# Hybrid decoder layer: the third and fourth right side of the MLP's up projection, tied on VectorE behind the second weights of its first two pairs

## The chip, the cores and the metric

The kernel runs on one core of a Trainium2 chip, as one program. The time is the device time of one execution in microseconds (us). Before the change it is 1497.02 us, the median of three executions (1496.89 to 1497.15).

The core has five engines with a queue of instructions each, and each works through its own queue in order: TensorE (PE in the profile, with its weight loads as PEld), VectorE (DVE), ScalarE (ACT), GpSimd (POOL) and SyncE (SP, which here issues every transfer). They meet at semaphores alone.

## The reference

One layer of a hybrid decoder on 1024 tokens of width 1024, all in float32. Ahead of the MLP stand an mLSTM and a forgetting attention side by side, and a cross attention into 256 memory tokens. The last part is

```python
        x = x + cross_attention(rmsnorm(x, ln_x[l]), rmsnorm(mem, ln_mem[l]), w_xq[l], w_xkv[l], w_xo[l])

        u = jax.nn.relu(rmsnorm(x, ln2[l]) @ w_ff1[l])
        x = x + (u * u) @ w_ff2[l]
    return rmsnorm(x, ln_f)
```

with `w_ff1` 1024 x 4096 and `w_ff2` 4096 x 1024. The change touches the step from the output projection of the cross attention (`w_xo`) into the up projection (`w_ff1`).

## The kernel before

**Numbers in two parts.** A float32 operand is kept as two tiles, `hi` and `lo`. `split` (L135) makes them: ScalarE copies the source into `hi` with rounding (L138), then VectorE subtracts `hi` from the source into `lo` (L139). A product is three matmuls, `lo*hi`, `hi*lo`, `hi*hi` (`mm3`, L221 to L223). So weights that come from memory cost one ACT and one DVE instruction of 128 x 1024 for each tile before TensorE can use them, and TensorE asks for the `lo` part first (L221).

**The up projection in seven products.** The normalised input (1024 x 1024, transposed) is cut into four blocks: y11 and y12 are the first 512 features for the first and the second 512 tokens, y21 and y22 the other 512 features. The weights are handled in 16 pairs of column tiles. For a pair, instead of eight block products seven are made, with sums and differences of blocks on both sides. The right sides (the table `RIGHTS`, L1474) are `11`, `21`, `t1`, `t2`, `22`, `t3` and `t4`, each an `act` tile of four k-slices of 512, hi and lo. Product i of pair p is called job (p, i) here. `jobs` (L1477) gives TensorE's order: for the first two pairs (0,1) (1,1) (0,2) (1,2) (0,5) (1,5) (0,6) (1,6) (0,3) (1,3) (0,7) (1,7) (0,4) (1,4). A job is four k-slices of three matmuls.

**Where the right sides come from.** `xo_sink` (L1506) adds each tile of `w_xo`'s output to the residual (L1509), squares it for the norm (ACT L258, DVE L262) and writes the scaled tile into `ys` (L1513). Right sides 11 and 21 are split while the first 512 tokens run, `t1` and `t2` (a `sub`, L1428, and a split for each k) while the second 512 tokens run, tile by tile (L1595, L1596). What is left then, in the list `rest` (L1612), is four splits for `22`, four times `third` and four times `fourth`:

- `third(k)`: y12 = y22 - y12 on VectorE (L1428), then a split into `t3` (ACT L138, DVE L139).
- `fourth(k)`: y21 = y21 - y11 on VectorE, then a split into `t4`.

`t3` is used first by job (0,7), `t4` by job (0,4): the last but one and the last product of a pair.

**Where the weights come from.** `left_up(p, group)` (L1449) makes the left sides of a pair in three groups: group 0 for jobs 1 and 2 (and 4), group 1 for jobs 5 and 6, group 2 for jobs 7 and 3. Each group is one 128 x 1024 split into tiles `wh` and `wl`, three buffers each for the whole kernel. "The second weights" are group 1. Group 0 of pair 1 adds five VectorE operations on 512 columns that build the sums (L1462 to L1467); from pair 2 on they run on GpSimd.

**What sets the order.** The program is recorded as the loops run; a scheduler then merges the recorded instructions into one queue for each engine, by priority in the order of recording, by readiness in its own estimate of time, and by free buffers. A manual dependence without a semaphore (`add_manual_dep` with `NoSync`) only says that one instruction has to stand behind another on an engine. The loop over jobs (L1723) records, ahead of each job, the weights of five jobs further on (`prepare`, L1491) and one or two entries of `rest`.

**Behind that stage**, `Pair.run` (L1629) adds up the products of a pair on VectorE (L1627), ScalarE makes relu and square (L1616, L1617), and `put_right` and `put` (L1663, L1670) split the results and write them to memory for the down projection, two DVE instructions of L139 and L1428 kind after another, while the next pairs run. The down projection (L1788) and the last part (L1865) follow.

Of the kernel before, what the change touches and what calls it, by code (L numbers as in the profile page):

```python
# [44 lines left out]
def hybrid_layer(ctx: ExitStack, tc: tile.TileContext, a: dict, out: bass.AP):  # L45
    nc = tc.nc
# [12 lines left out]
    def sb(tag, shape, bufs, dt=F32):  # L59
        return pool.tile(shape, dt, tag=tag, name=name(tag), bufs=bufs)  # L60
# [18 lines left out]
    def w2(tag, n=512, dt=F32, p=P):  # L79
        return sb("r_" + tag, [P, 512], BUFS[tag], dt)[:p, :n]  # L80
# [54 lines left out]
    def split(hi, lo, src, scale=None):  # L135

        if scale is None:
            s.activation(hi, src, AF.Copy)  # L138
            return v.tensor_tensor(out=lo, in0=src, in1=hi.bitcast(F32), op=ALU.subtract)  # L139
        else:  # L140
            s.activation(hi, src, AF.Copy, scale=scale)
            return v.scalar_tensor_tensor(out=lo, in0=src, scalar=scale, in1=hi.bitcast(F32), op0=ALU.mult, op1=ALU.subtract)
# [82 lines left out]
    def both(pair, f):  # L225
        return f(pair[0]), f(pair[1])
# [77 lines left out]
    at = 0  # L304
# [950 lines left out]
    fourth = []  # L1255
# [171 lines left out]
    def sub(out_, x, y, by=v):  # L1427
        by.tensor_tensor(out=out_, in0=x, in1=y, op=ALU.subtract)  # L1428
# [8 lines left out]
    def raw_pair(p_, n0, n1):  # L1437
        raws = [sb("wr", [P, 1024], 2) if p_ % 2 else z4()[:, :1024] for _ in range(2)]
        if p_ > 1:
            n0, n1 = n1, n0  # L1440
        for raw, n in zip(raws, (n0, n1)):
            load(raw, a["w_ff1"][n])
        return raws[::-1] if p_ > 1 else raws

    todo = [(b, k, 4 * b + k, 4 * b + 2 + k) for b in range(NB) for k in range(2)]

    cuts = {}

    def left_up(p_, group):  # L1449

        if group == 0:
            raws[p_] = raw_pair(p_, *todo[p_][2:])
        r1, r2 = raws[p_]
        x11, x12, x21, x22 = r1[:, :TH], r1[:, TH:], r2[:, :TH], r2[:, TH:]
        hi, lo = (sb(t, [P, 1024], 3, F32R) for t in ("wh", "wl"))
        split(hi, lo, (r1, r2, r1)[group])
        if group == 0:
            h22, l22 = (w2(t, dt=F32R) for t in ("bc" if p_ else "ay"))
            split(h22, l22, x22)
            cuts[p_, 4] = both((h22, l22), lambda t: t.rearrange("p (k c) -> p k c", k=4))  # L1460

            by = g if p_ > 1 else v  # L1462
            by.tensor_tensor(out=x21, in0=x21, in1=x22, op=ALU.add)
            sub(x22, x21, x11, by)
            sub(x12, x12, x22, by)
            sub(x11, h22.bitcast(F32), x22, by)
            by.tensor_tensor(out=x11, in0=x11, in1=l22.bitcast(F32), op=ALU.add)  # L1467
        for e in range(2):
            cuts[p_, ((1, 2), (5, 6), (7, 3))[group][e]] = both((hi, lo), lambda t: t[:, e * TH : e * TH + TH].rearrange("p (k c) -> p k c", k=4))
        if group == 2:  # L1470
            del raws[p_]
# [11 lines left out]
    first = {}  # L1483
# [7 lines left out]
    def prepare(at):  # L1491
        while prep and first[prep[0]] <= at + LEAD:
            left_up(*prep.pop(0))

    def cut_h(c, hf, ks=range(4)):
        k0 = 4 if c in ("21", "22", "t4") else 0
        for k in ks:
            ins = split(H[c][0][:, k], H[c][1][:, k], ys[hf][k0 + k])
        return ins
# [86 lines left out]
    for n in range(KT):  # L1586
        w = weights(a["w_xo"][n])
        if n == 1:
            norm_factors(0)
        if n in (1, 7):  # L1590
            left_up(*prep.pop(0))
        for _, _, ps in proj(w, os_, 1, order=[(1, 0)]):
            xo_sink(n, 1, ps)
        k = n % 4
        sub(ys[0][k], ys[1][n], ys[0][k])  # L1595
        cut_h("t2" if n > 3 else "t1", 0, (k,))  # L1596
# [3 lines left out]
    def third(k):  # L1600
        y12, y22 = parts[1][k], parts[3][k]
        sub(y12, y22, y12)
        cut_h("t3", 1, (k,))

    def fourth(k):

        y11, y21 = parts[0][k], parts[2][k]
        sub(y21, y21, y11)
        cut_h("t4", 0, (k,))


    rest = [lambda k=k: cut_h("22", 1, (k,)) for k in range(4)] + [lambda k=k: third(k) for k in range(4)] + [lambda k=k: fourth(k) for k in range(4)]  # L1612

    def squared(x, y):

# [105 lines left out]
    pairs = {}  # L1721
    later = []
    for at, (p_, i) in enumerate(jobs):  # L1723
# [14 lines left out]
        if i == 4:  # L1738
            b, k = todo[p_][:2]
# [207 lines left out]
```

## Time and profile before

| | value |
|---|---|
| median of three executions | 1497.02 us |
| profiled execution: its own time | 1498.83 us |
| profiled execution: span of the trace | 1497.1 us, 22496 instructions |
| PE busy | 1479.4 us, 99% of the span |
| PEld busy | 1253.1 us, 84% |
| DVE busy | 1131.0 us, 76% |
| ACT busy | 773.1 us, 52% |
| POOL busy | 521.2 us, 35% |
| granted TensorE clock | 0.998 |

Of a profile row in time order, the first number is the start in us from the span's start, the second the duration, then engine, line, operation, output and inputs by the program's names without buffer numbers; in brackets stands the idle time of that engine just before, and who ended it. Neighbouring rows of one form are merged (x2). The end of a matmul is modelled and overlaps the next one, so a gap between matmuls is read from their starts. The output projection of the second 512 tokens runs until about 849 us of the span, the up projection from about 841 us to past 1150 us, and the down projection after it.

### The profile page before, as it was taken

What the parts mean: (1) busy time and instruction counts of PE and PEld (TensorE: products, weight loads), DVE (VectorE), ACT (ScalarE), POOL (GpSimd) and SP (SyncE); (2) the same over time, 40 slices, a digit from 0 to 9 for tenths busy, and PEclk for the clock granted to TensorE, in tenths of its full rate; (3) what the DMA queues carried; (4) which work ended last, traced back from release to release, by engine and by line L of the source; (5) the groups of instructions that cost most, each with busy time, mean ns of one, the idle gap of its engine ahead of it and who ended that gap; (6) DMA issues with size and microseconds to landing.
All of it is one profiled execution on the core that took longest, in us unless ns stands there. A gap on an engine that the chain in (4) does not pass through costs nothing. (4 is left out here: it accounts for less than half of the span.)

```text
span 1497.1 us, 22496 instructions
## 1 busy us (share of the span) xinstructions
PE 1479.4 (99%) x7790; PEld 1253.1 (84%) x7790; DVE 1131.0 (76%) x1867; ACT 773.1 (52%) x1492; POOL 521.2 (35%) x552
## 2 busy tenths in 40 slices
PE   9999999999999999999999999999999999999997
PEld 9988888889999888889988787888888888888887
DVE  7775776776798875677668888999996677787665
ACT  7434353445688664577644557666665521222134
POOL 1002020414456441633200045454544365553312
PEclk9999999999999999999999999999999999999999
DMA  6422333446778867744544447776678767776623
GB/s 231 138 95 69 130 97 134 132 132 191 247 242 284 285 231 247 261 168 128 167 165 155 139 171 268 253 246 238 233 267 304 264 260 281 281 274 253 250 87 113
DMA packets 125878, 303.58 MB, mean 203 GB/s; under 512 B 14898, under 2 KB 30060, under 8 KB 118852
## 3 DMA queue, kind: packets, MB, share of 16 engines
q1 hardware_dynamic: 125764, 302.15, 57.9%
q8 instruction: 61, 1.00, 0.3%
q14 instruction: 53, 0.43, 0.1%
HBM read 203.28 MB, written 98.82 MB: 202 GB/s over the span
## 5 line engine op out<-in xcount | busy, mean ns | idle before, releaser
L221 PE MATMUL tp<-act,wl 128*128 128x512 f32 (+1 forms) x440 | 172.7, 392 | 0.0
L222 PE MATMUL tp<-act,wh 128*128 128x512 f32 (+1 forms) x440 | 172.2, 391 | 0.0
L223 PE MATMUL tp<-act,wh 128*128 128x512 f32 (+1 forms) x440 | 171.7, 391 | 0.0
L139 DVE TENSOR_TENSOR wl<-wr,wh 128x1024 fp32r<-128x1024 f32 (+2 forms) x99 | 131.8, 1331 | 29.0 <-ACT wh L138 28.7
L138 ACT ACTIVATE wh<-wr 128x1024 fp32r<-128x1024 f32 (+2 forms) x99 | 99.9, 1010 | 86.3 <-PE tp L223 28.9
L221 PE MATMUL mm<-act,wl 128*128 128x512 f32 (+1 forms) x332 | 123.7, 373 | 0.0
L223 PE MATMUL mm<-act,wh 128*128 128x512 f32 (+1 forms) x332 | 123.5, 372 | 0.0
L222 PE MATMUL mm<-act,wh 128*128 128x512 f32 (+1 forms) x332 | 123.5, 372 | 0.0
L221 PE MATMUL m<-act,wl 128*128 128x512 f32 (+1 forms) x308 | 113.9, 370 | 1.8 <-DVE wl L139 1.8
L223 PE MATMUL m<-act,wh 128*128 128x512 f32 (+1 forms) x308 | 113.7, 369 | 0.0
L222 PE MATMUL m<-act,wh 128*128 128x512 f32 (+1 forms) x308 | 113.4, 368 | 0.0
L223 PE MATMUL sc<-act,wh 128*128 128x512 f32 (+1 forms) x280 | 105.6, 377 | 0.0
L221 PE MATMUL sc<-act,wl 128*128 128x512 f32 (+1 forms) x280 | 105.5, 377 | 0.0
L222 PE MATMUL sc<-act,wh 128*128 128x512 f32 (+1 forms) x280 | 105.5, 377 | 0.0
L223 PEld LDWEIGHTS tp<-act,wh 128*128 128x128 f32 x440 | 82.7, 188 | 18.6
L221 PEld LDWEIGHTS tp<-act,wl 128*128 128x128 f32 x440 | 82.7, 188 | 18.5 <-DVE r_f L1627 0.2
L222 PEld LDWEIGHTS tp<-act,wh 128*128 128x128 f32 x440 | 82.8, 188 | 18.2
L1711 POOL TENSOR_TENSOR z<-wr 128x256 f32<-128x256 f32 x56 | 50.1, 915 | 135.6 <-DMA wr<-w_ff2q 133.1
L138 ACT ACTIVATE wh<-z 128x1024 fp32r<-128x1024 f32 (+1 forms) x54 | 55.4, 1026 | 79.0 <-POOL z L1711 58.4
L139 DVE TENSOR_TENSOR wl<-z,wh 128x1024 fp32r<-128x1024 f32 (+1 forms) x54 | 79.3, 1468 | 9.3 <-ACT wh L138 9.3
L138 ACT ACTIVATE w<-wr 128x768 fp32r<-128x768 f32 (+3 forms) x35 | 28.1, 802 | 109.5 <-PE tp L221 33.5
L223 PEld LDWEIGHTS mm<-act,wh 128*128 128x128 f32 x332 | 62.4, 188 | 11.7
(793 smaller groups left out, 4398.5 us busy)
## 6 DMA issues: line engine op xcount, KB each, us to landing
act<-right SPq DMA_DIRECT2D x49, 1024.0 KB
right<-w SPq DMA_DIRECT2D x56, 256.0 KB
wr<-w_ff2q SPq DMA_DIRECT2D x28, 512.0 KB
right<-r_d SPq DMA_DIRECT2D x49, 256.0 KB
right<-r_e SPq DMA_DIRECT2D x49, 256.0 KB
act<-fqk SPq DMA_DIRECT2D x48, 256.0 KB
wr<-w_in SPq DMA_DIRECT2D x20, 512.0 KB
wr<-w_ff SPq DMA_DIRECT2D x20, 512.0 KB
```

The costliest lines, as they stand in the source:

```text
L138: s.activation(hi, src, AF.Copy)
L139: return v.tensor_tensor(out=lo, in0=src, in1=hi.bitcast(F32), op=ALU.subtract)
L221: nc.tensor.matmul(ps, w[1], x[0], start=first, stop=False, skip_group_check=more)
L222: nc.tensor.matmul(ps, w[0], x[1], start=False, stop=False, skip_group_check=more)
L223: nc.tensor.matmul(ps, w[0], x[0], start=False, stop=last, skip_group_check=more)
L1711: g.tensor_tensor(out=o, in0=x, in1=y, op=op)
```

## The change

`left_up` now keeps, for each pair and group, the VectorE instruction that writes the `lo` tile. The eight entries of `rest` for `third` and `fourth` are recorded through a new function, which adds a manual dependence without a semaphore from each of their VectorE instructions to the `lo` instruction of pair 1, group 1. Only VectorE's instructions are tied. No instruction is added or taken away.

```diff
-    cuts = {}
+    cuts, cut_of = {}, {}
...
-        split(hi, lo, (r1, r2, r1)[group])
+        cut_of[p_, group] = split(hi, lo, (r1, r2, r1)[group])
...
+    def later_than(cut, do):
+        at = len(nc.cur_bb.bb.instructions)
+        do()
+        for i in nc.cur_bb.bb.instructions[at:]:
+            if i.engine == mybir.EngineType.DVE:
+                tc.add_manual_dep(
+                    i,
+                    cut_of[cut].ins.name,
+                    mybir.DependencyInfo(mybir.DependencyClass.NoSync, mybir.DependencyReason.DATA),
+                    reason="behind the weights of the first pairs",
+                )
+
-    rest = [lambda k=k: cut_h("22", 1, (k,)) for k in range(4)] + [lambda k=k: third(k) for k in range(4)] + [lambda k=k: fourth(k) for k in range(4)]
+    rest = [lambda k=k: cut_h("22", 1, (k,)) for k in range(4)] + [lambda f=f, k=k: later_than((1, 1), lambda: f(k)) for f in (third, fourth) for k in range(4)]
```

The scheduler then plans everything behind that point anew. Three places of VectorE's queue show it. In the rows the last number of a name is the tile's own number; lines above L1612 stand 12 higher in the changed file (L1627 is L1639).

VectorE before, up to the `lo` part of pair 0's group 1 (`wl_9589`), which job (0,5) asks for. `act_9585` is `t3`, `act_9586` is `t4`, `act_9200` is `t2`:

```order
L1428 TENSOR_TENSOR w_1680_9154<-w_1680_9154,w_1653_8987 128x512
L139 TENSOR_TENSOR act_9585<-w_1694_9237,act_9585 128x512
L1509 TENSOR_TENSOR r_p_9572<-mm_9547,r_p_9572 128x512
L139 TENSOR_TENSOR act_9585<-w_1694_9237,act_9585 128x512
L1428 TENSOR_TENSOR wr_9530<-wr_9530,wr_9531 128x512
L1428 TENSOR_TENSOR wr_9530<-r_b_9538,wr_9531 128x512
L139 TENSOR_TENSOR act_9200<-w_1653_8987,act_9200 128x512
L139 TENSOR_TENSOR act_9585<-r_d_9347,act_9585 128x512
L139 TENSOR_TENSOR wl_9589<-z_1700_9257,wh_9588 128x1024
```

Now the nine rows of `third` and `fourth` that stood ahead of `wl_9589` are gone from there, and VectorE's queue behind it reads, from the `lo` part of pair 1's group 1 (`wl_9593`) on:

```order
L139 TENSOR_TENSOR wl_9593<-wr_9531,wh_9592 128x1024
L1428 TENSOR_TENSOR w_1694_9237<-r_f_9433,w_1694_9237 128x512
L1428 TENSOR_TENSOR w_1694_9237<-r_d_9476,w_1694_9237 128x512
L1428 TENSOR_TENSOR r_d_9347<-r_e_9519,r_d_9347 128x512
L1428 TENSOR_TENSOR r_e_9390<-r_f_9579,r_e_9390 128x512
L1428 TENSOR_TENSOR w_1666_9070<-w_1666_9070,w_1635_8871 128x512 x2
L1428 TENSOR_TENSOR w_1680_9154<-w_1680_9154,w_1653_8987 128x512 x2
L139 TENSOR_TENSOR act_9200<-w_1653_8987,act_9200 128x512
L139 TENSOR_TENSOR act_9585<-w_1694_9237,act_9585 128x512 x2
L139 TENSOR_TENSOR act_9585<-r_d_9347,act_9585 128x512
L139 TENSOR_TENSOR act_9585<-r_e_9390,act_9585 128x512
L1639 TENSOR_TENSOR w_1773_9686<-m_1772_9673,row 128x512
```

Nine instructions left the place ahead of `wl_9589`: six differences (L1428) and three splits of `t3`. All eight differences now follow `wl_9593`, then the splits. Two splits of `t4` (`act_9586`) and `wl_9646`, the `lo` part of pair 0's group 2 for job (0,3), come next. Up to `wl_9646` the queue holds the same work as before but for one split of `t4` and a small norm instruction (L1520), which moved behind it; up to `wl_9911` (pair 3, group 0) it holds exactly the same work.

Further on the plan differs too. VectorE ahead of `wl_10426`, pair 6, group 0, before:

```order
L139 TENSOR_TENSOR w_1854_10281<-w_1854_10281,r_e_10629 128x512
L139 TENSOR_TENSOR r_f_10331<-r_f_10331,r_d_10608 128x512
L1627 TENSOR_TENSOR r_p_10221<-tp_10318,r_p_10221 128x512
L139 TENSOR_TENSOR r_c_10430<-z_1872_10421,r_b_10429 128x512
L139 TENSOR_TENSOR wl_10426<-z_1873_10422,wh_10425 128x1024
L1627 TENSOR_TENSOR r_f_10501<-tp_10488,r_p_10396 128x512
L1428 TENSOR_TENSOR w_1895_10568<-w_1895_10568,r_p_10221 128x512
L139 TENSOR_TENSOR w_1895_10568<-w_1895_10568,r_e_10673 128x512
```

and now:

```order
L139 TENSOR_TENSOR r_c_10430<-z_1872_10421,r_b_10429 128x512
L139 TENSOR_TENSOR w_1854_10281<-w_1854_10281,r_e_10571 128x512
L139 TENSOR_TENSOR w_1854_10281<-w_1854_10281,r_e_10629 128x512
L1428 TENSOR_TENSOR w_1895_10568<-w_1895_10568,r_p_10221 128x512
L139 TENSOR_TENSOR r_p_10221<-r_p_10221,r_d_10653 128x512
L139 TENSOR_TENSOR w_1895_10568<-w_1895_10568,r_e_10673 128x512
L139 TENSOR_TENSOR wl_10426<-z_1873_10422,wh_10425 128x1024
```

Three instructions that prepare the results of pair 4 for memory now stand ahead of the weights of pair 6. The same three-row move comes again at pairs 9 and 12; at pairs 4 and 7 four such rows moved behind the weights instead. TensorE's queue keeps the order of its jobs for the first two pairs, with a few matmuls of neighbouring jobs exchanged.

## The prediction

> **What bounds the kernel now.** I read the page's busy times first, then TensorE's waits over the whole span, then the stretches of time, then queue by queue the two places that the waits name.
>
> ```profile
> span 1497.1 us, 22496 instructions
> PE 1479.4 (99%) x7790; PEld 1253.1 (84%) x7790; DVE 1131.0 (76%) x1867; ACT 773.1 (52%) x1492; POOL 521.2 (35%) x552
> PE m L221 <- DVE wl L139: 1.8, 2, 1.6
> PE mm L248 <- DVE c_r L1853: 1.6, 1, 1.6
> 800.00:900.00 100.00, 98.42 (x431) 79.36 (x430) 88.16 (x123) 51.13 (x78) 17.48 (x10) 1.00 0.46 157
> 900.00:1000.00 100.00, 99.78 (x429) 80.07 (x428) 90.94 (x100) 68.11 (x109) 49.75 (x30) 1.00 0.74 257
> 1000.00:1100.00 100.00, 100.00 (x430) 80.30 (x428) 91.26 (x98) 64.07 (x101) 47.42 (x30) 1.00 0.69 240
> ```
>
> TensorE bounds the kernel: 99% busy. The third row is its wait for weights (1.8 us in 2 waits, the longest 1.6); the fourth lies in the end phase, which the change leaves alone. In the windows (PE is the first figure behind the length, DVE the third) TensorE issues some 430 matmuls per 100 us through the up projection, one each 0.233 us; the only holes from 800 to 1100 us are the two waits of the third row. VectorE is 88 to 91% busy beside it, so what is moved on VectorE can turn into a wait of TensorE. In time order:
>
> ```profile
> 855.54 0.40 PE L223 MATMUL tp<-act,wh 128*128 128x512 f32 x1
> 857.52 0.50 PE L221 MATMUL m<-act,wl 128*128 128x512 f32 x1 [1.58 <-DVE wl L139]
> 857.86 0.40 PE L222 MATMUL m<-act,wh 128*128 128x512 f32 x1
> 872.51 0.39 PE L221 MATMUL m<-act,wl 128*128 128x512 f32 x1
> 903.26 0.27 PE L285 MATMUL mm<-ident,gcol 128*8 128x128 f32 x1
> 903.76 0.50 PE L221 MATMUL m<-act,wl 128*128 128x512 f32 x1 [0.22 <-DVE wl L139]
> ```
>
> The first pair of rows is job (0,5) asking for `wl_9589`. From start to start stand 1.98 us where 0.233 would do, and the next start follows 0.34 later, not 0.233: the wait costs 1.75 + 0.10 = **1.85 us**. The row at 872.51 is job (0,3), which needs `wl_9646`. The last row is job (3,1) waiting for `wl_9911`, 0.22 + 0.10 = 0.32 us.
>
> ```profile
> 843.19 0.69 DVE L1463 TENSOR_TENSOR wr<-wr 128x512 f32<-128x512 f32 x1 [0.17 <-DMA wr<-w_ff]
> 844.81 1.23 DVE L139 TENSOR_TENSOR wl<-wr,wh 128x1024 fp32r<-128x1024 f32 x1 [0.92 <-ACT wh L138]
> 845.95 0.74 DVE L1513 SCALAR_TENSOR_TENSOR r_e<-r_p,vec,row 128x512 f32<-128x512 f32 x1
> 846.61 0.69 DVE L139 TENSOR_TENSOR r_c<-wr,r_b 128x512 fp32r<-128x512 f32 x1
> ...
> 855.64 0.69 DVE L139 TENSOR_TENSOR act<-r_d,act 128x512 fp32r<-128x512 f32 x1
> 856.24 1.23 DVE L139 TENSOR_TENSOR wl<-z,wh 128x1024 fp32r<-128x1024 f32 x1
> 868.09 1.21 DVE L139 TENSOR_TENSOR wl<-z,wh 128x1024 fp32r<-128x1024 f32 x1
> 871.54 0.69 DVE L1627 TENSOR_TENSOR r_f<-ov,row 128x512 f32<-128x512 f32 x1 [0.29 <-PE ov L223]
> 872.71 0.69 DVE L1627 TENSOR_TENSOR r_f<-sc,row 128x512 f32<-128x512 f32 x1 [0.48 <-PE sc L223]
> 875.03 1.74 DVE L139 TENSOR_TENSOR wl<-z,wh 128x1024 fp32r<-128x1024 f32 x1 [0.50 <-ACT wh L138]
> 878.74 1.29 DVE L1428 TENSOR_TENSOR w<-r_f,r_p 128x512 f32<-128x512 f32 x1 [1.36 <-ACT r_f L1617]
> 893.61 0.69 DVE L1428 TENSOR_TENSOR w<-w,row 128x512 f32<-128x512 f32 x1 [1.36 <-ACT row L1617]
> 902.49 1.22 DVE L139 TENSOR_TENSOR wl<-wr,wh 128x1024 fp32r<-128x1024 f32 x1
> ```
>
> This is VectorE's queue. From starts: 0.60 us for 512 columns (855.64 to 856.24), 1.14 for a weight split (844.81 to 845.95), 0.66 for L1513. From 844.81 on it runs without a hole until the 0.29 us ahead of 871.54, so the row at 856.24, `wl_9589`, came late because of what stood ahead of it.
>
> **The change, part by part.** No instruction is added, removed or given a semaphore wait; no transfer is added. All depends on places in queues.
>
> *The wait at job (0,5).* In the new order stand between L1463 and `wl_9589`: L1513, one weight split, and eleven instructions of 512 columns. From the landing of the weights at 843.19, which the change does not touch, that is 0.60 + 0.66 + 1.14 + 11 x 0.60 = 9.0 us: `wl_9589` starts at 852.2 and is there at 853.4. Its `wh` must be there too:
>
> ```profile
> 850.07 1.05 ACT L138 ACTIVATE wh<-z 128x1024 fp32r<-128x1024 f32 x1
> 855.98 1.06 ACT L138 ACTIVATE wh<-wr 128x1024 fp32r<-128x1024 f32 x1 [1.93 <-PE tp L223]
> ```
>
> It is written by 851.1 even in the old order, where three ACT splits of `t3` stand ahead of it. TensorE reaches job (0,5) at 855.54 + 0.23 = 855.77. There are 2.3 us to spare, so the whole wait goes: **-1.85 us**. It could be less only if VectorE lost over 2.3 us on the way.
>
> *What now comes later.* VectorE goes on behind `wl_9589` with five instructions, then `wl_9593`, which cannot start before its `wh`: the second row above, 855.98 + 1.06, held by TensorE's job (0,2), not by VectorE. So `wl_9593` runs from 857.1 to 858.2; TensorE asks for it in job (1,5), 33 matmuls after 855.77, at 863.5. Then eight differences, one split of `t2`, four of `t3`, one L1627 and two splits of `t4`, 16 x 0.60 = 9.6 us, then `wl_9646`: 867.8 to 869.0. GpSimd works beside it:
>
> ```profile
> 861.08 3.56 POOL L1463 TENSOR_TENSOR z<-z 128x512 f32<-128x512 f32 x1 [129.59 <-DMA z<-w_ff]
> 865.86 1.68 POOL L1463 TENSOR_TENSOR wr<-wr 128x512 f32<-128x512 f32 x1 [1.22 <-DVE w L1428]
> 863.99 1.20 DVE L139 TENSOR_TENSOR act<-r_f,act 128x512 fp32r<-128x512 f32 x1
> 866.31 1.78 DVE L139 TENSOR_TENSOR act<-r_e,act 128x512 fp32r<-128x512 f32 x1
> 869.89 0.68 DVE L139 TENSOR_TENSOR r_c<-z,r_b 128x512 fp32r<-128x512 f32 x1
> ```
>
> Beside those two POOL rows, two splits took 1.20 and 1.78 us in place of 0.69: 1.6 us more. With that, `wl_9646` is there between 869.0 and 870.6. TensorE, 1.85 us early, asks at 872.51 - 1.85 = 870.66. A wait of 0 to 0.5 us; I take **+0.1**.
>
> The Trainium skill, page "SBUF — State Buffer", section "Who interferes with whom", says that a DVE instruction with two inputs in SBUF contends with a GpSimd instruction that reads SBUF, and that whoever issues second is blocked until the other ends. The trace agrees that such a split is slowed, though not that it always waits for a whole instruction (0.51 us beside one of 3.56). It speaks against the change, since all the moved instructions have two SBUF inputs. By the rule in its strict form the sum below would be 0.8 us larger.
>
> *The wait at job (3,1).* Up to `wl_9911` VectorE has the same work as before, and a wait of TensorE that is gone does not make VectorE's work less. Between `wl_9646` and `wl_9911` lay 902.49 - 868.09 = 34.4 us, of which 4.0 idle: 0.29 and 0.48 behind TensorE, 0.50 and twice 1.36 behind ACT. Work is 30.4, plus 0.7 for what moved behind `wl_9646`. From a start of `wl_9646` at 867.8 to 869.4, with none to all of the idle time, `wl_9911` is there at 867.8 + 31.1 + 1.2 = 900.1 at the earliest and 869.4 + 31.1 + 4.0 + 1.2 = 905.7 at the latest; TensorE comes at 903.54 - 1.85 = 901.69. The wait lies between 0 and 4.1 us (with 0.10 for the restart), in place of 0.32: a term of -0.3 to +3.8. The holes tied to TensorE go, as it comes sooner; of those behind ACT's relu the new order fills the first and half of the second. I take half of the idle time as staying, from the middle of the start: 868.6 + 31.1 + 2.0 + 1.2 = 902.9, a wait of 1.3, so **+1.0**.
>
> *The later pairs.* At pairs 6, 9 and 12 three instructions now stand ahead of group 0's `lo` part. Pair 6 in the trace:
>
> ```profile
> 958.64 2.21 DVE L139 TENSOR_TENSOR wl<-z,wh 128x1024 fp32r<-128x1024 f32 x1 [0.26 <-ACT wh L138]
> 961.38 1.47 DVE L1428 TENSOR_TENSOR w<-w,r_p 128x512 f32<-128x512 f32 x1
> 962.88 1.67 DVE L139 TENSOR_TENSOR w<-w,r_e 128x512 fp32r<-128x512 f32 x1
> 967.32 0.68 DVE L139 TENSOR_TENSOR r_p<-r_p,r_d 128x512 fp32r<-128x512 f32 x1
> 962.66 0.39 PE L221 MATMUL sc<-act,wl 128*128 128x512 f32 x1
> ```
>
> The weights were there at 960.9 and used at 962.66: 1.8 us spare. The three cost 3 x 0.60 = 1.8 undisturbed and 1.38 + 1.58 + 0.60 = 3.6 as they ran here beside GpSimd. So 0 to 1.8 us late at each, 0 to 5.4 in all; VectorE has small holes there to draw on, so I take near the low end, **+0.4**. At pairs 4 and 7, where four rows moved the other way, TensorE had no wait to lose, so they give nothing.
>
> Behind 904 us TensorE had no wait until the end phase, so what it gains passes through to the end. Sum: -1.85 + 0.1 + 1.0 + 0.4 = **-0.35 us**. The profiled execution took 1498.83 us, 1.7 more than its span of 1497.1 and 1.8 more than the median 1497.02; the sum is a difference and goes onto the median: **1496.7 us**.
>
> **Rivals.**
>
> *Everything is kept*: no wait at `wl_9646`, `wl_9911` or the later pairs, and the old 0.32 goes too. -1.85 - 0.32 = -2.2: 1494.9. For it: 4.0 us of idle time ahead of `wl_9911`. Against: VectorE's unchanged work.
>
> *All is paid back at job (3,1)*: the 4.0 us stay. -1.85 + 0.1 + 3.8 = +2.05: 1499.1.
>
> *Slower, through the later pairs*: from the point where the three moved instructions cost over the 1.8 us spare, TensorE waits at pairs 6, 9 and 12. At the full 1.8 each: -1.85 + 0.1 + 0.3 + 5.4 = +4.0: 1501.0. For it: GpSimd is 47 to 50% busy in the windows there, and the two rows of 1.47 and 1.67. Against: a VectorE that falls behind once has more room at the next pair.
>
> *Moved instructions blocked by GpSimd*: if the eight differences and the splits meet POOL's two L1463 for their whole 1.3 us each (the short ones of its rows), 2.6 in place of 1.6, `wl_9646` comes at 871.6 and TensorE waits 0.9 us there, 0.8 more than taken: 1497.5.
>
> *The change doesn't do what it says*: `wl_9589` waits for ACT, not for its place, and the wait stays: 1497.0. The row at 850.07 speaks against it.
>
> **How the numbers follow.** Forecast (1495.6 to 1498.2) 0.48; everything kept 0.17; paid back 0.12; blocked 0.07; the later pairs 0.13; no effect 0.03. The likeliest is 1496.7. The range runs from 1494.8, the full gain, to 1500.3, which leaves out the upper part of the later pairs. With 0.2% being 3.0 us, about what a measurement of this kernel can tell from no change, faster means under 1494.0: the waits in reach add up to 2.2 us, so 0.03. Slower, over 1500.0, is most of the later pairs' case and a tail of "paid back": 0.12. The same: 0.85.
>
> **What would show it.** The wait of 1.58 at "PE m L221" gone, with `wl` some 3 to 4 us earlier: the first step right. A wait of about 1 us at the job that uses `wl` near 902 us: the third step; none: "everything kept". New rows "PE sc L221" or "PE ov L221" waiting for "DVE wl L139" near 962, 1022 and 1081 us: the later pairs. The forecast is wrong if the sum of PE's waits between 840 and 1150 us changes by over 3 us, or if the time moves while they don't.

## The result, and the profile after

The changed kernel takes 1502.15 us (median of 6 executions, 1501.36 to 1507.2), the kernel before 1496.95 on the same chip: a ratio of 1.0042 [1.0028, 1.0055], 5.2 us slower. Forecast were 1496.7 us, with a range up to 1500.3, and a chance of 0.12 for slower. A second set of executions of the same two kernels gave 1502.28 against 1496.94 us, 1.0038 [1.0024, 1.0051]. Two of the eleven executions of e7 below took 2082 and 2084 us at a granted clock of 0.65, the profiled one among them; only its other nine are used.

Where the time lies is read from two landmarks that all the kernels here share: the L262 row of VectorE for the norm at about 821 us, ahead of the change's place, and the first one at about 1445 us, behind the down projection. VectorE's rows, of the kernel before

```profile
822.11 0.69 DVE L262 TENSOR_TENSOR r_b<-r_c,r_b 128x512 f32<-128x512 f32 x1
...
1447.07 0.69 DVE L262 TENSOR_TENSOR r_b<-r_c,r_b 128x512 f32<-128x512 f32 x1 [0.70 <-ACT r_c L258]
```

and of the changed kernel:

```profile
820.92 0.69 DVE L262 TENSOR_TENSOR r_b<-r_c,r_b 128x512 f32<-128x512 f32 x1
...
1450.35 0.69 DVE L262 TENSOR_TENSOR r_b<-r_c,r_b 128x512 f32<-128x512 f32 x1 [0.70 <-ACT r_c L258]
```

The stretch between them is 624.96 us before and 629.4 after: 4.5 us of the loss lie there. Ahead of it the two profiled executions differ by 1.2 us the other way (822.11 and 820.92), though the queues are the same up to there; that is most of why the spans (1497.1 and 1500.8 us) differ by less than the medians. TensorE's waits from 840 to 1160 us in the changed kernel (us in total, times, longest):

```profile
PE m L221 <- DVE wl L139: 3.1, 2, 1.8
PE sc L221 <- DVE w L1639: 1.2, 1, 1.2
PE tp L221 <- DVE r_f L1639: 0.8, 2, 0.4
```

and the same waits in TensorE's queue:

```profile
871.42 0.50 PE L221 MATMUL m<-act,wl 128*128 128x512 f32 x1 [1.79 <-DVE wl L139]
...
890.59 0.50 PE L221 MATMUL sc<-act,r_c 128*128 128x512 f32 x1 [1.17 <-DVE w L1639]
...
905.59 0.50 PE L221 MATMUL m<-act,wl 128*128 128x512 f32 x1 [1.32 <-DVE wl L139]
...
945.43 0.50 PE L221 MATMUL tp<-act,wl 128*128 128x512 f32 x1 [0.37 <-DVE r_f L1639]
```

The wait at job (0,5), 1.58 near 857 us, is gone. In its place stand a wait at job (0,3) for `wl_9646` (871.42), one at job (1,4) for an addition of L1639 that frees its PSUM tile (890.59), one at job (3,1) for `wl_9911` (905.59), and two of 0.4 (the second at 1122.80). All five end with VectorE. Its queue in the changed kernel:

```profile
835.19 0.69 DVE L1509 TENSOR_TENSOR r_p<-m,r_p 128x512 f32<-128x512 f32 x1 [0.39 <-PE m L223]
...
836.59 1.22 DVE L139 TENSOR_TENSOR wl<-wr,wh 128x1024 fp32r<-128x1024 f32 x1
...
843.47 0.69 DVE L1463 TENSOR_TENSOR wr<-wr 128x512 f32<-128x512 f32 x1 [1.98 <-DMA wr<-w_ff]
...
852.50 1.22 DVE L139 TENSOR_TENSOR wl<-z,wh 128x1024 fp32r<-128x1024 f32 x1
...
857.17 1.22 DVE L139 TENSOR_TENSOR wl<-wr,wh 128x1024 fp32r<-128x1024 f32 x1 [0.26 <-ACT wh L138]
858.32 1.79 DVE L1428 TENSOR_TENSOR w<-r_f,w 128x512 f32<-128x512 f32 x1
...
861.83 3.59 DVE L1428 TENSOR_TENSOR w<-w,w 128x512 f32<-128x512 f32 x4
...
870.16 1.21 DVE L139 TENSOR_TENSOR wl<-z,wh 128x1024 fp32r<-128x1024 f32 x1
...
878.35 1.36 DVE L139 TENSOR_TENSOR wl<-z,wh 128x1024 fp32r<-128x1024 f32 x1 [1.50 <-ACT wh L138]
...
904.32 1.22 DVE L139 TENSOR_TENSOR wl<-wr,wh 128x1024 fp32r<-128x1024 f32 x1
```

`wl_9589` starts at 852.50, forecast was 852.2; `wl_9646` starts at 870.16, forecast were 867.8 to 869.4. But the whole profile runs 1.2 us earlier here, so both came later than they look: counted from the L1509 row at 835.19 (836.38 in the kernel before), which follows TensorE, `wl_9589` came 17.3 us behind it, where 15.8 was forecast. Three things are to be seen. VectorE waits 1.98 us at 843.47 for pair 1's weights, where it had waited 0.17. Of the eight differences behind `wl_9593` (858.32 to 865.35, 7.03 us for what takes 8 x 0.60 = 4.8) the first takes 1.79 and the four at 861.83 take 3.59 in place of 2.4: they lie beside GpSimd's two L1463, which now run here:

```profile
857.49 2.06 POOL L1463 TENSOR_TENSOR z<-z 128x512 f32<-128x512 f32 x1 [127.14 <-DMA z<-w_ff]
862.17 1.50 POOL L1463 TENSOR_TENSOR wr<-wr 128x512 f32<-128x512 f32 x1 [2.61 <-DMA wr<-w_ff]
```

And the wait at 843.47 has its reason on SP, which the prediction did not look at. VectorE frees the buffer for pair 1's second weight tile with a weight split. That split and the anchor used below, of the kernel before:

```profile
836.38 0.69 DVE L1509 TENSOR_TENSOR r_p<-m,r_p 128x512 f32<-128x512 f32 x1
...
837.52 1.22 DVE L139 TENSOR_TENSOR wl<-wr,wh 128x1024 fp32r<-128x1024 f32 x1 [0.45 <-ACT wh L138]
```

SP's own queue of the kernel before, and behind it that of the changed kernel:

```profile
838.77 0.33 SPq L1442 DMA_DIRECT2D wr<-w_ff  x1
839.59 0.86 SPq L1508 DMA_DIRECT2D r_p<-x1d  x1
```

```profile
835.91 0.32 SPq L1510 DMA_DIRECT2D x2d<-r_p  x1
838.32 0.32 SPq L1508 DMA_DIRECT2D r_p<-x1d  x1
838.73 0.84 SPq L1442 DMA_DIRECT2D wr<-w_ff  x1
```

Before, the load is issued as soon as the split ends (837.52 + 1.22 = 838.74). Now the buffer is free at 836.59 + 1.22 = 837.81, but the load of the last residual tile stands ahead on SP, and that one waits for the store of 835.91 and is issued at 838.32 only, 2.4 us behind it. Counted from the same L1509 row, the load goes out at 3.54 us where it was 2.39, and VectorE's L1463 starts at 8.28 where it was 6.81: 1.5 us later against TensorE.

### The profile page after: what moved, and what is told of

It is laid out like the page before. It is cut to its first block, busy times and chain, and to the rows that moved or that the text cites. A ratio compares the mean times of both kernels' runs of the same rounds, so it can differ in the third digit from the quotient of the medians.

```text
span 1500.8 us, 22503 instructions
## 1 busy us (share of the span) xinstructions
PE 1480.7 (99%) x7790; PEld 1253.0 (83%) x7790; DVE 1134.1 (76%) x1867; ACT 773.2 (52%) x1492; POOL 521.9 (35%) x552
```

## The experiments

The three theories weighed first: **A**: VectorE had idle time ahead of 845 us that four of the eight differences used to fill; tied, they stand in a stretch without idle time, and TensorE pays. **B**: the splits of `t3` and `t4` that stand ahead of `wl_9646` cost. **C**: the scheduler's new order of jobs from pair 3 on costs. After the first four runs came **D**: the late load alone costs; and **E**: GpSimd beside VectorE is the larger part. Each run was timed in five rounds beside the kernel before on the same chip. The last column is the stretch between the two L262 rows in the profiled execution.

| run | median us | before, same chip | ratio | stretch us |
|---|---|---|---|---|
| before (again) | 1496.90 | 1496.94 | 0.9996 [0.9988, 1.0005] | 624.96 (623.75) |
| changed (again) | 1502.28 | 1496.94 | 1.0038 [1.0024, 1.0051] | 629.42 (628.27) |
| e1 splits tied alone | 1497.26 | 1497.38 | 0.9997 [0.9988, 1.0006] | 623.46 |
| e2 differences tied | 1505.31 | 1497.38 | 1.0051 [1.0038, 1.0063] | 628.50 |
| e3 `fourth` behind (0,2) | 1500.20 | 1497.38 | 1.0018 [1.0009, 1.0027] | 626.90 |
| e4 `third` alone | 1500.07 | 1497.38 | 1.0016 [1.0007, 1.0025] | 626.14 |
| e5 changed, load first | 1500.36 | 1496.51 | 1.0035 [1.0021, 1.0049] | 626.84 |
| e6 before, load second | 1496.38 | 1496.51 | 0.9998 [0.9989, 1.0007] | 623.23 |
| e7, e14 four differences less | 1497.61, 1497.34 | 1496.51, 1496.97 | 1.0006 [0.9997, 1.0016], 0.9998 [0.9989, 1.0007] | 624.79 (e14) |
| e11 changed, GpSimd less | 1497.82 | 1496.94 | 1.0006 [0.9997, 1.0015] | 623.80 |
| e13 before, GpSimd less | 1496.68 | 1496.97 | 0.9997 [0.9988, 1.0006] | 623.70 |
| e8, e12 splits behind (1,1), (0,2) | 1495.55, 1495.91 | 1496.51, 1496.94 | 0.9994 [0.9985, 1.0003], 0.9988 [0.9980, 0.9997] | 622.51, 622.49 |

### e1: the splits alone

```diff
-            if i.engine == mybir.EngineType.DVE:
+            if i.engine == mybir.EngineType.DVE and i is not nc.cur_bb.bb.instructions[at]:
```

> Only the eight splits (L139) of `third` and `fourth` are tied; the eight differences (L1428) are free again. Up to `wl_9911` VectorE's queue then holds from the first L1463 row on 73 instructions, as before the change, and not 77; ahead of `wl_9589` it holds 16 (19 before, 14 with the change). Theory A (the loss comes from the differences: four of them used to fill idle time of VectorE ahead of 845 us, and tied they stand in a stretch without idle time): no wait of TensorE for `wl` between 840 and 910 us of more than 0.3, the old 1.8 gone, 1.5 to 2.3 us below the kernel before. Theory B (the loss comes from the splits of `t3` and `t4` that stand between `wl_9593` and `wl_9646`): seven of the eight still stand there, so a wait of 1 to 2 us at job (0,3) stays, within 1 us of the kernel before. Theory C (the loss comes from the new order of the jobs and of VectorE's rows from pair 3 on): TensorE's order is that of the kernel before here, so 1.5 to 2.3 us below it, and A and C are not told apart by this run.

Measured: no loss. VectorE's queue (L1509, L1463, `wl_9646`, `wl_9911`):

```profile
835.40 0.69 DVE L1509 TENSOR_TENSOR r_p<-m,r_p 128x512 f32<-128x512 f32 x1
...
841.96 0.68 DVE L1463 TENSOR_TENSOR wr<-wr 128x512 f32<-128x512 f32 x1
...
866.98 1.21 DVE L139 TENSOR_TENSOR wl<-z,wh 128x1024 fp32r<-128x1024 f32 x1
...
900.12 1.22 DVE L139 TENSOR_TENSOR wl<-wr,wh 128x1024 fp32r<-128x1024 f32 x1
```

L1463 starts 6.56 us behind the anchor, without a wait for its load, and `wl_9911` 64.7 us behind it (66.1 before, 69.1 with the change). TensorE has no wait for `wl`, though seven splits of `t3` and `t4` stand between `wl_9593` and `wl_9646`: B, which expected a wait of 1 to 2 us there, falls by that. By the median alone it would not: 0.1 us below the kernel before lies in B's range, and A had 1.5 to 2.3 below. The stretch is 1.5 us shorter than in the first profile of the kernel before, as A said, but only 0.3 us shorter than in the second, told below.

### e2: the differences alone

```diff
-        for i in nc.cur_bb.bb.instructions[at:]:
+        for i in nc.cur_bb.bb.instructions[at : at + 1]:
```

> Only the eight differences are tied; the splits follow them as they depend on them. Up to `wl_9911` the queue of VectorE has the counts of the changed kernel (14, 37 and 77 instructions ahead of `wl_9589`, `wl_9646` and `wl_9911`). Theory A: the whole loss is here, 4 to 6 us above the kernel before, with waits of 1 to 2 us at jobs (0,3) and (3,1). Theory B (ties of the splits): it is the ties of the splits that cost, so with them gone less than half of the loss stays, 0 to 2.5 us above. Theory C: as the changed kernel, 4 to 6 us above, since the later plan is nearly that of the changed kernel.

This edit did more than the expectation says: the same line stands in two older helpers (`behind`, L167, and `ahead_of`, L182), and they were changed too, so this program's order differs from about 600 us on, and it is no clean test. Made in `later_than` alone, the edit gives the changed kernel's program, instruction for instruction, so it has no run of its own: tying the differences is all that the change does. What e2 measured is 7.9 us above the kernel before, of which its stretch holds 3.5. It showed something else, told in the last section.

### e3: `fourth` behind `wl_9646`; e4: `third` alone

```diff
-[lambda f=f, k=k: later_than((1, 1), lambda: f(k)) for f in (third, fourth) for k in range(4)]
+[lambda k=k: later_than((1, 1), lambda: third(k)) for k in range(4)] + [lambda k=k: later_than((0, 2), lambda: fourth(k)) for k in range(4)]
```

> `third` stays tied behind `wl_9593`; `fourth` is tied behind `wl_9646` (pair 0, group 2) instead, so that 31 instructions and not 37 stand ahead of `wl_9646`, but still 76 ahead of `wl_9911`; the later plan is nearly that of the changed kernel. Theory A (VectorE's lost idle time): the wait at (0,3) goes, but the debt is paid at (1,4) and (3,1): 1.5 to 4 us above the kernel before. Theory B (only the place of `wl_9646`): the loss goes with the wait there, 0 to 2 us below the kernel before. Theory C (later plan): the loss stays for the most part, 3 to 5 us above.

```diff
+[lambda k=k: later_than((1, 1), lambda: third(k)) for k in range(4)] + [lambda k=k: fourth(k) for k in range(4)]
```

> Only `third` is tied; `fourth` is free. Ahead of `wl_9589`, `wl_9646` and `wl_9911` stand 15, 40 and 75 instructions (before: 19, 35, 73; changed: 14, 37, 77), and TensorE's order from pair 3 on is that of the kernel before. Theory A: half of the differences are lost to the idle time (2 x 0.60 us and what GpSimd adds), `wl_9646` is as late as in the changed kernel or later: 1 to 4 us above the kernel before, waits at (0,3) and (3,1). Theory B: `wl_9646` stands three places later than in the changed kernel, so its wait there grows to 2 to 3.5 us: 1 to 3 us above. Theory C: with the old later plan the loss is gone: 0 to 2 us below the kernel before.

In e3 the wait at (0,3) is gone, but 1.04 at (3,1) and others stay: 2.8 us above the kernel before, within A's range and not in B's. Its interval (1.3 to 4.0 us) reaches into C's, so C is left to e4. In e4 TensorE's order from pair 3 on is that of the kernel before, and 2.7 us are lost all the same, with waits of 1.16 at (0,3) and 0.87 at (3,1): C falls.

### e5 and e6: the order of two loads on SP

```diff
+        if hf == 1 and n == KT - 1:
+            tc.add_manual_dep(
+                res.ins,
+                last_raw_up[0].ins.name,
...
```

`res` is the load of the last residual tile (L1508), `last_raw_up[0]` that of pair 1's second weight tile. In e6 the two names change places, in the kernel before.

> The changed kernel, with one order on SP put back: the load of pair 1's second weight tile (L1442 in the kernel before, `wr<-w_ff`) is tied ahead of the load of the last residual tile (L1508, `r_p<-x1d`), as in the kernel before. In the changed kernel it stood behind it and was issued 1.15 us later against TensorE (3.54 us behind the start of the L1509 row, 2.39 before), and VectorE stood idle 1.98 us for it. Theory A (VectorE's lost idle time, four differences of 0.60 us in a full stretch): VectorE starts again 1.2 to 1.6 us earlier, but still has 77 instructions to do ahead of `wl_9911`: 2.5 to 4.5 us above the kernel before. Theory D (the late load alone makes the loss): at most 1.5 us above it, with waits for `wl` below 0.5.

> The kernel before, with that one order on SP turned round: the load of pair 1's second weight tile stands behind the load of the last residual tile. Theory D: VectorE, which has no idle time behind it, is 1.0 to 1.6 us later at `wl_9589`, and the wait of 1.58 at job (0,5) grows by as much: 1 to 2 us above the kernel before. Theory A: the order of two loads costs little by itself, since VectorE has differences to do while it waits: 0 to 0.7 us above.

e5 stays 3.9 us above the kernel before. VectorE's wait for the load falls to 0.65 us, and TensorE's wait at (0,3) from 1.79 to 0.49, but the one at (3,1) keeps its 1.32:

```profile
841.44 0.69 DVE L1465 TENSOR_TENSOR wr<-wr 128x512 f32<-128x512 f32 x1 [0.65 <-DMA wr<-w_ff]
...
869.43 0.50 PE L221 MATMUL m<-act,wl 128*128 128x512 f32 x1 [0.49 <-DVE wl L139]
902.71 0.50 PE L221 MATMUL m<-act,wl 128*128 128x512 f32 x1 [1.32 <-DVE wl L139]
```

In e6 the load goes out as late as in the changed kernel (at 838.53, 3.5 us behind the L1509 row) and nothing is lost. VectorE's queue there:

```profile
838.56 1.29 DVE L1428 TENSOR_TENSOR w<-r_d,w 128x512 f32<-128x512 f32 x2
839.77 0.69 DVE L1428 TENSOR_TENSOR w<-w,w 128x512 f32<-128x512 f32 x1
...
841.76 1.23 DVE L139 TENSOR_TENSOR wl<-wr,wh 128x1024 fp32r<-128x1024 f32 x1
842.90 0.69 DVE L1465 TENSOR_TENSOR wr<-wr 128x512 f32<-128x512 f32 x1
```

VectorE does differences while the weights come, and then the row at 841.76, the split of pair 1's first weights: the scheduler moved it ahead of L1463 (here L1465), behind which it stands in the kernel before. VectorE stands idle nowhere from 837.3 to 869 us. So e6 turned more round than the two loads; it shows that a late load can be hidden, not that the differences alone hide it. D falls by e5, where the load is early and 3.9 of the 5.3 us stay, and by e7 and e14 below, where it is late and at most 1.1 stay. The late load's own part of the 5.3 is about 1.5 us by the medians, and 1.4 or 2.6 by the stretches (e5 against the two profiles of the changed kernel).

### e7 and e14: four differences less

```diff
-        sub(y12, y22, y12)
+        if k > 1:
+            sub(y12, y22, y12)
...
-        sub(y21, y21, y11)
+        if k > 1:
+            sub(y21, y21, y11)
```

> The changed kernel without the differences of k = 0 and 1 of `third` and of `fourth` (y12 and y21 are split as they are, so `t3` and `t4` are wrong there): the four that the kernel before did ahead of 843 us. Up to `wl_9911` VectorE's queue holds 73 instructions, as in the kernel before, and 33 up to `wl_9646`; the load of pair 1's second weight tile stays in its late place. Theory A: nearly all of the loss goes, 1.5 us below to 1.5 us above the kernel before. Theory D: the late load still costs, 2.5 to 5 us above.

> The changed kernel without the four differences of k = 0 and 1 (y12 and y21 are split as they are there), once more for its trace. If the debt is those four: `wl_9911` starts 2.4 us earlier against the L1509 row at 835 us than in the changed kernel (66.7 in place of 69.1 us), the waits for `wl` between 860 and 910 us sum to less than 1 us (3.1 in the changed kernel), and the stretch between the L262 rows is 624 to 626 us (629.4). If it is not: waits of over 2 us, and 627 us or more.

1.1 and 0.4 us above the kernel before, in place of 5.3. VectorE's rows in e14 (L1463, `wl_9911`) and TensorE's only wait for `wl` from 840 us on:

```profile
843.76 0.69 DVE L1463 TENSOR_TENSOR wr<-wr 128x512 f32<-128x512 f32 x1 [2.52 <-DMA wr<-w_ff]
...
901.06 1.22 DVE L139 TENSOR_TENSOR wl<-wr,wh 128x1024 fp32r<-128x1024 f32 x1
```

```profile
PE m L221 <- DVE wl L139: 0.3, 1, 0.3
```

`wl_9911` starts 66.1 us behind the anchor of 834.96, as in the kernel before (69.1 with the four), though VectorE waits 2.52 us for the late load.

The four are those that the kernel before does between 833 and 842 us. Four instructions of 0.60 us, 2.4 us of VectorE's time, carry most of the loss. The other runs fit this when they are put in order by the number of instructions from L1463 to `wl_9911`: with 73 (before, e1, e7, e8, e14) they lie between 1.0 us below and 1.1 above the kernel before, with 75 (e4) 2.7 above, with 76 (e3) 2.8, with 77 (e5, changed) 3.9 and 5.3. The exception is e11 below, with 77 and 0.9 above, which leaves out work of GpSimd.

### e9 and e10: both kernels a second time

> The kernel before, profiled a second time, to see what of its first profile is the rule. Its first profiled execution had lost 1.0 to 1.9 us more ahead of 822 us than six profiles of kernels whose program is the same up to there. If the wait at job (0,5) is the rule: 1.4 to 1.8 us there again, with the rows ahead of 822 us some 1.4 us earlier, median within 0.5 us of the kernel before. If it is not: under 0.8 us, and a kernel that takes this wait away can gain no more than that.

> The changed kernel, profiled a second time. Theory A (VectorE is late by a debt that does not depend on the execution): the same three places again, waits of 1 to 2 us at jobs (0,3), (1,4) and (3,1), 4 to 6 us above the kernel before. If the waits are those of one execution: other places, and a median that differs by over 2 us from the first one's 5.2 above.

TensorE in the second profile of the kernel before, and in that of the changed kernel:

```profile
855.81 0.50 PE L221 MATMUL m<-act,wl 128*128 128x512 f32 x1 [1.01 <-DVE wl L139]
```

```profile
871.56 0.50 PE L221 MATMUL m<-act,wl 128*128 128x512 f32 x1 [1.54 <-DVE wl L139]
904.75 0.50 PE L221 MATMUL m<-act,wl 128*128 128x512 f32 x1 [1.32 <-DVE wl L139]
```

The wait at (0,5) was 1.01 this time and not 1.58, between the two cases of the expectation, and the 0.22 at (3,1) was not there. So the first profile overstated what there was to gain, by some 0.8 us, and lay 1.9 us above its median to begin with. The waits at (0,3) and (3,1) of the changed kernel came again; the one at (1,4) shrank to 0.19. Both kernels' stretches are some 1.2 us shorter in the second profile. First against first and second against second they differ by 4.46 and 4.52 us; taken crosswise, by 3.3 and 5.7.

### e11 and e13: GpSimd taken away

```diff
             by = g if p_ > 1 else v
+            if p_ in (2, 3):
+                by = type('N', (), {'tensor_tensor': staticmethod(lambda **_: None)})
```

> The changed kernel without GpSimd's five operations (L1463 to L1467) for pairs 2 and 3, whose sums are left out, so that VectorE's differences and splits between 857 and 910 us run with hardly any GpSimd beside them; 14, 37 and 77 instructions stand ahead of `wl_9589`, `wl_9646` and `wl_9911` as in the changed kernel. Theory A with the four differences alone (2.4 us): the loss shrinks by the 2.2 us that the differences lost beside GpSimd at most, and 2 to 4 us stay. Theory E (GpSimd is the larger part: 2.2 us at the differences and some 5 us in the rows of 1.5 to 2.2 us from 880 to 890 us): waits of less than 0.5 in all between 860 and 910 us, 1.5 us below to 1 us above the kernel before.

> The kernel before without GpSimd's five operations (L1463 to L1467) for pairs 2 and 3, whose sums are left out: the counterpart of the same cut in the changed kernel, which took 4.4 us off it. If GpSimd's work beside VectorE is hidden in the kernel before (VectorE has idle time to spend there, and TensorE has no wait behind job (0,5) up to 1160 us): within 0.7 us of the kernel before, the stretch between the L262 rows at 821 and 1445 us 623 to 625 us. If GpSimd's work costs the kernel before as much as the changed one: 3 to 5 us below it.

In the changed kernel this takes 4.5 us away: 1497.82. VectorE's rows there (`wl_9593`, four differences, `wl_9646`):

```profile
856.96 1.23 DVE L139 TENSOR_TENSOR wl<-wr,wh 128x1024 fp32r<-128x1024 f32 x1 [0.25 <-ACT wh L138]
...
860.51 2.49 DVE L1428 TENSOR_TENSOR w<-w,w 128x512 f32<-128x512 f32 x4
...
867.73 1.22 DVE L139 TENSOR_TENSOR wl<-z,wh 128x1024 fp32r<-128x1024 f32 x1
```

From `wl_9593` to `wl_9646` pass 10.77 us in place of 12.99: GpSimd costs 2.2 us there. In the kernel before it gains nothing that can be measured (1496.68 against 1496.97); VectorE only stands idle longer in front of TensorE, 1.64 us where it was 0.29:

```profile
870.50 0.69 DVE L1629 TENSOR_TENSOR r_f<-ov,row 128x512 f32<-128x512 f32 x1 [1.64 <-PE ov L223]
```

So E holds by its number, but not as a cause beside A: GpSimd's share is hidden as long as VectorE has time in hand, and becomes TensorE's once it has not. Taking away either the four differences or GpSimd's work brings nearly the whole loss back; the shares do not add up, since TensorE pays only what goes beyond VectorE's reserve.

### e8 and e12: a better version

The splits alone are tied, as in e1, those of `third` behind `wl_9593` and those of `fourth` behind `wl_9646`; the differences are free.

```diff
-            if i.engine == mybir.EngineType.DVE:
+            if i.engine == mybir.EngineType.DVE and i is not nc.cur_bb.bb.instructions[at]:
...
+[lambda k=k: later_than((1, 1), lambda: third(k)) for k in range(4)] + [lambda k=k: later_than((0, 2), lambda: fourth(k)) for k in range(4)]
```

> As with the splits alone tied, but those of `fourth` behind `wl_9646`: 16, 34 and 73 instructions ahead of `wl_9589`, `wl_9646` and `wl_9911`, the differences free, the load of the weights in its old place. Theory A and D both: no wait for `wl` between 840 and 910 us, 1.4 us less from 822 us to the end of the down projection than before, so 0.5 to 2.3 us below the kernel before. If a gain in the trace does not show in the median, between 0.5 below and 0.5 above.

> The kernel with only the splits tied, those of `fourth` behind `wl_9646`, a second time, for its interval: no wait for `wl` between 840 and 910 us. If the wait at job (0,5) is the rule in the kernel before, 0.7 to 1.8 us below it; if it is not, within 0.5.

1.0 us below the kernel before both times; the second interval (0.9980 to 0.9997) leaves out 1, the first (0.9985 to 1.0003) just not. The gain is small, but it has the size of the wait that is gone (1.01 and what TensorE takes to start again, 1.3 in all; the stretch is 1.26 shorter than in the second profile of the kernel before). TensorE's waits in e12 from 600 us on:

```profile
PE mm L248 <- DVE c_r L1865: 1.6, 1, 1.6
PE sc L1859 <- POOL r_b L262: 0.5, 1, 0.5
PE sc L221 <- DVE r_c L142: 0.2, 1, 0.2
```

None is for `wl`; the first two lie in the end phase. It beats the changed kernel by 6 us.

## Why the prediction was wrong

**The wait at job (0,5), -1.85.** Right in its mechanism: the wait went. `wl_9589` came 1.5 us later than forecast against TensorE (17.3 us behind the L1509 row, not 15.8), which the 2.3 us to spare took up; that 852.50 looks like the forecast of 852.2 is luck. The size of the wait was that of one execution; the second profile had 1.01 + 0.27 = 1.3 (0.27 is what 1.85 had over the 1.58 shown, and is added to every wait here).

**"The landing of the weights at 843.19, which the change does not touch."** This step failed first. The plan exchanged two loads on SP, and VectorE started 1.5 us later against TensorE. The scheduler's new order for SP showed it; the walk along VectorE took the landing as fixed. It is not the whole: with the load back in its place (e5) 3.9 of the 5.3 us stay.

**The wait for `wl_9646`, +0.1 (0 to 0.5).** Mis-sized: 1.79 + 0.27 = 2.1. From the L1509 row the walk's middle gave 868.6 - 836.38 = 32.2 us; measured were 870.16 - 835.19 = 35.0. Of the 2.8 us the load made 1.5, and GpSimd 1.4: it took 2.2 us from the moved instructions, where the sum took the middle of 0 to 1.6, with the old durations of splits that stood beside it only in part.

**The wait at job (3,1), +1.0 (-0.3 to +3.8).** Near in size, 1.32 - 0.22 = +1.1, and that is luck. From the L1509 row the forecast has `wl_9911` start 65.3 us behind in the middle and 68.1 at the latest; it came 69.1 behind, out of its range. The wait stayed near the forecast because TensorE was late too, by two waits ahead of it. One of them, 1.17 at (1,4) (1.4 with the restart), was in no term: a late VectorE holds up not only the weights, but also the additions of L1639 that free PSUM. In the second profile it was 0.19, so its size goes by the execution.

**The later pairs, +0.4 (0 to 5.4).** The rival "slower, through the later pairs" had the right sign and not the right place: no wait for `wl` at pairs 6, 9 or 12. Two waits of 0.4 for L1639 rows remain there, 1.3 in all.

The measured terms sum to -1.85 + 2.1 + 1.1 + 1.4 + 1.3 = +4.1 us, against 4.5 in the stretch. At job (3,1) TensorE waits for `wl_9911` in the first profiles of both kernels, so what it has lost by then is what VectorE is late by, however the waits ahead share it out: 69.1 - 66.1 = 3.0 us. "All is paid back at job (3,1)" was the nearest rival in kind: its reason, that a wait of TensorE that is gone does not make VectorE's work less, is what happened, at three jobs in place of one. "Blocked by GpSimd" had the right neighbour and 0.8 us; measured were 2.2 us in all at that place, 1.4 more than the sum had. The strict rule of the Trainium skill, page "SBUF — State Buffer", section "Who interferes with whom", gave 0.8 us more than the sum: nearer to the trace at the differences (2.2 us), and still far from the total.

What stands behind it: ahead of 845 us the moved differences cost nothing. From 833 us on the kernel before stands idle there for 0.45, 0.17 and 0.92 us (1.5 in all), the changed one for 0.70, 0.39, 0.70, 0.39 and 1.98 (4.2). Four differences, 2.4 us, had filled those holes and now stand where VectorE has none. The forecast's walk did count them there, but paid for them with idle time and with rows slowed by GpSimd that it expected to shrink: by its middle `wl_9911` came 0.8 us sooner behind the landing than before (58.5 us against 59.3), and it took 60.9. Work that is taken out of a place where an engine waits anyway is not moved, it is added.

## What to carry to other kernels

Before a step is tied behind something, look whether it fills idle time of its engine where it stands. If it does, tie only its part that is in the way (here the splits, 1.0 us faster than before) and leave the part that fills the hole free (the differences, whose tie made the 5.3 us). Walk through the new order of every queue that feeds the anchor of the estimate, SP's too, before a landing is taken as fixed.

## What the runs showed of the hardware

**Behind a wait of about 2 us TensorE's clock can fall.** In e2 the wait at job (0,3) was 2.01 us, and 0.8 us behind its end TensorE's clock fell to half for some 3.4 us. Two rows of the windows (the last three figures are the granted clock, the DMA share and GB/s) and TensorE's queue:

```profile
877.00:878.00 1.00, 1.00 (x4) 0.81 (x3) 1.00 (x3) 0.00 (x0) 0.00 (x0) 0.50 0.81 311
880.00:881.00 1.00, 1.00 (x6) 0.81 (x5) 1.00 (x2) 0.91 (x1) 0.83 (x1) 1.00 0.31 45
```

```profile
875.66 0.50 PE L221 MATMUL m<-act,wl 128*128 128x512 f32 x1 [2.01 <-DVE wl L139]
...
877.29 0.63 PE L223 MATMUL m<-act,wh 128*128 128x512 f32 x1
877.71 0.63 PE L221 MATMUL m<-act,wl 128*128 128x512 f32 x1
```

From start to start stand 0.42 us there in place of 0.233, for eight matmuls: 1.5 us more. The same came behind e2's wait of 2.16 us near 631 us. In the traces of all the executions that are used the clock falls nowhere else ahead of the end phase. It did not come behind the 1.79 of the changed kernel, nor behind waits of 2.12 and 2.25 near 645 us in the profiles of the kernel before and of e13. The Trainium skill, page "TensorE: Matmul & The Clock Gate", section "Part 1: The HAM clock gate (the "warmup" mystery)", gives an idle window of some 3.4 us as what halves the clock; here both falls followed a wait of about 2 us. That the wait is their cause is likely but not shown, since longer waits passed without one. That such falls make the longest of the changed kernel's executions (1507.2 us, at a mean clock of 0.996 where the profiled ones have 0.997 and 0.998) is a guess; it was not profiled.

**GpSimd's price for VectorE depends on who has time.** The same five operations for two pairs cost the changed kernel 4.5 us and the kernel before nothing that could be measured (0.9997 [0.9988, 1.0006] without them).
